# Later splits of the small products' operands and earlier w_out sums of odd pairs in a short-convolution block

## The chip, the cores and the metric

The kernel runs on one core of a Trainium2 chip. The metric is the device time of one execution in microseconds; runs are compared by their median. The profile comes from one execution that the hardware profiler recorded. TensorE (PE, and PEld for its weight loads) multiplies, VectorE (DVE) and ScalarE (ACT) work on SBUF and PSUM, GpSimd (POOL) works on SBUF alone, and SyncE (SP) issues nearly all DMAs. Each of them works through its own instructions in order.

## The reference

With DEPTH = 1 only the first layer, a gated short convolution between two norms, is computed, for 1024 positions of 1024 channels and an inner width of 2048, all in float32.

```python
def short_conv_mixer(u, w_in, conv_w, w_out):
    z, bg, cg, v = jnp.split(u @ w_in.astype(u.dtype), 4, axis=-1)
    y = bg * causal_dwconv(cg * v, conv_w) * jax.nn.silu(z)
    return y @ w_out.astype(u.dtype)
...
    u = rms_norm(h, pre_norm[i])
    m = short_conv_mixer(u, sc_w_in[j], sc_conv_w[j], sc_w_out[j])
    h = h + rms_norm(m, post_norm[i])
```

## The kernel before

Every float32 operand is split into a high and a low float32r part (`split`, L153: ScalarE copies the high part, VectorE subtracts to get the low part), and a product is three matmuls, low by high, high by low and high by high. The head normalises and transposes x into u. Then come the input projections, chunk by chunk. The 16 chunks of 128 inner channels give 32 **pairs** p: an even pair holds the columns of cg and v of chunk p // 2, an odd pair those of z and bg. One pair is a two by two block product, done with seven block products named a to g instead of eight. Each is 4 x 3 matmuls of 128x512 (L188 to L190). GpSimd makes the sums of weight blocks (`add_s`, L142 to L150), `split_w` splits them, and `after` combines the results: ScalarE copies a, c and e out of PSUM (`snap`, L196, tiles sna, snc, sne), and VectorE adds later products to them (L215 for d, L220 for f, L229 and L230 for g). Products a, g, c and d of one pair use one PSUM bank (px), so the next product on that bank waits until the snap of a has been read.

From chunk DEEP = 3 on (pair 6), the eighth product b is itself done with seven **small products** a' to g' (L684 to L686, 2 x 3 matmuls of 128x256) for the two pairs of a chunk together. Their u side is prepared once: `deep_parts` and `deep_subs` form sums on GpSimd, and `deep_split` splits them, c' with two copies and two subtractions of 128x256, and likewise e', d' and g'. This happens in the products of pairs 4 to 6, as the table `UNDER` (L755) says. Their weights come from `deep_sums` (GpSimd, L647 to L651) and `deep_prep` (tiles dw). `deep_after` (L695) adds a small product into sna; behind d' it calls `start_conv`, which multiplies into gpad (L236) and runs `conv`: one ScalarE copy (L578) and two VectorE sums of 128x1024 (L580).

The order of work is written out by hand in `slots` (L737). An even pair runs as c a' e b' d f c', then a of the next pair, e', g; an odd pair as c f' e d' d f g', then a of the next pair, g. Behind every product's matmuls the loop issues `prepare`, which splits the weights of the products that are due within LEAD = 7 us of a fixed table, then `after` or `deep_after`, then the DMAs and sums that belong to that product. An engine works in the order of this code, so a step's place in the loop is its place in its engine's queue.

Four sums of w_out (`add_t`, L278) are also made in this loop, for the output projection later. For each of eight row blocks, listed in `TODO` under the pairs 8, 10, 12, 13, 14, 15, 16 and 17, `fetch_t` (L272) loads four tiles t of 256 KB with four DMAs on SP. Four VectorE subtractions (L282, steps 0 to 3) follow, each with a store to DRAM (L283). In an even pair the loads stand behind c and all steps behind d. In an odd pair the loads stand behind c and the steps one by one behind d, f, the next a, and g:

```python
        if i in "dfag" and p % 2 != (i == "a") and p - (i == "a") in TODO:
            add_t(TODO[p - (i == "a")], ["dfag".index(i)])
```

Raw weights of pair p + 2 are fetched behind d (`fetch`, L130, four DMAs on SP). `y_done` (L243) stores a chunk of y behind g of an odd pair, on SP too. Pages of SBUF come from one pool of 36; a new tile takes a page that was freed earlier, and waits for it. The output projection, the second norm and the residual follow (L843 on).

Of the kernel before, what the change touches and what calls it, by code (L numbers as in the profile page):

```python
# [16 lines left out]
DEEP = 3  # L17
# [4 lines left out]
def kernel(  # L22
# [48 lines left out]
    def page(name, dtype=F32, shape=(HB,)):  # L71

        return pages.tile([P, *shape], dtype, tag="pg", name=name, bufs=PAGES)
# [79 lines left out]
    def split(src, hi, lo):  # L153
        nc.scalar.copy(hi, src)  # L154
        nc.vector.tensor_sub(lo, src, hi.bitcast(F32))  # L155
# [21 lines left out]
    def product(p, i, ks=None):  # L177

        w = wt[p, i]
        which = {"b": "y", "e": "v", "f": "v"}.get(i, "x")  # L180
        first = i in "abe"
        if first and (p, which) not in banks:
            banks[p, which] = bank(f"p{which}_{p}")
        ps = banks[p, which]
        for k in range(KH) if ks is None else ks:
            hi, lo = (h[:, k * P : (k + 1) * P] for h in w)
            last = k == KH - 1
            nc.tensor.matmul(ps, lo, UH[i][:, k], start=first and k == 0, stop=False, skip_group_check=True)  # L188
            nc.tensor.matmul(ps, hi, UL[i][:, k], start=False, stop=False, skip_group_check=True)  # L189
            nc.tensor.matmul(ps, hi, UH[i][:, k], start=False, stop=last, skip_group_check=True)  # L190
# [8 lines left out]
    def tap(c, j):  # L199
        i = j * NC + c  # L200
        return cw[:, i : i + 1]
# [30 lines left out]
            elif c < DEEP:  # L232
                start_conv(c)

    def start_conv(c):
        nc.vector.tensor_mul(gpad[:, TAPS - 1 : TAPS - 1 + HB], banks[2 * c, "x"], sn[2 * c, "a"])  # L236
        conv(c)


    done = {}  # L240
# [5 lines left out]
    def fetch_s(c):  # L246

        if c >= CH:
            ts = [page(f"s{e}_{c}") for e in (0, 1)]
            for e in (0, 1):  # L250
                nc.sync.dma_start(ts[e], y_d[:, c - CH, e * HB : (e + 1) * HB])
            done[c] = done[c], *ts
# [19 lines left out]
    def fetch_t(j):  # L272

        ts[j] = [page(f"t{n}_{j}") for n in range(4)]
        for n, t in enumerate(ts[j]):
            nc.sync.dma_start(t, wov[:, j + n // 2 * CH, n % 2 * HB : (n % 2 + 1) * HB])

    def add_t(j, steps=range(4)):  # L278

        t = ts[j]  # L280
        for n, a, b in [((1, 1, 0), (3, 3, 1), (0, 3, 0), (2, 2, 3))[n] for n in steps]:
            nc.vector.tensor_sub(t[n], t[a], t[b])  # L282
            nc.sync.dma_start(t_d[:, n, j], t[n])  # L283
# [289 lines left out]
    add_s(2, "ecdf")  # L573
    fetch(3)

    def conv(c):
        cv = tmp.tile([P, L], F32, tag="cv", name=f"cv_{c}")
        nc.scalar.activation(cv, gpad[:, :L], AF.Copy, scale=tap(c, 0))  # L578
        for j in range(1, TAPS):
            nc.vector.scalar_tensor_tensor(  # L580
                cv, gpad[:, j : j + L], tap(c, j), cv, op0=ALU.mult, op1=ALU.add
            )
        cvs[c] = cv
# [33 lines left out]
    def deep_subs(ks):  # L617

        for k in ks:
            (b11, b12), (b21, b22) = ((t[:, :HH], t[:, HH:]) for t in (deep[k], deep[k + KQ]))  # L620
            nc.gpsimd.tensor_sub(b12, b12, b11)
            nc.gpsimd.tensor_sub(b22, b22, b12)
            nc.gpsimd.tensor_sub(b11, b22, b11)
            nc.gpsimd.tensor_sub(b21, b21, b22)
# [3 lines left out]
    def deep_split(i):  # L628

        k0, l0 = DEEP_U[i]  # L630
        ls = slice(l0, l0 + HH)
        if i != "e'":
            deep[i] = [tmp.tile([P, KQ, HH], F32R, tag="ub", name=f"u{i[0]}{h}_deep", bufs=6) for h in "hl"]
        for k in range(KQ):
            if i == "e'":
                hi, lo = UH["b"][:, k, ls], UL["b"][:, k, ls]
            else:
                hi, lo = (t[:, k] for t in deep[i])
            split(deep[k0 + k][:, ls], hi, lo)

    def deep_sums(c, part):

        (a11, a12), (a21, a22) = ((t[:, :HH], t[:, HH:]) for t in (block(p, 0, 1) for p in (2 * c, 2 * c + 1)))
        t = page(f"ds{part}_{c}")
        deep[c, part] = t
        if part == 0:
            nc.gpsimd.tensor_add(t[:, :HH], a21, a22)  # L647
            nc.gpsimd.tensor_sub(t[:, HH:], t[:, :HH], a11)
        else:
            nc.gpsimd.tensor_sub(t[:, :HH], a11, a21)  # L650
            nc.gpsimd.tensor_sub(t[:, HH:], a12, deep[c, 0][:, HH:])  # L651
# [17 lines left out]
    def deep_product(c, i):  # L669

        n, off = DEEP_W[i]
        which = {"b'": "y'", "e'": "v'", "f'": "v'"}.get(i, "x'")
        first = i in ("a'", "b'", "e'")
        if first:
            banks[c, which] = bank(f"p{which[0]}2_{c}")
        ps = banks[c, which][:, :HH]
        for k in range(KQ):
            hi, lo = (h[:, off + k * P : off + (k + 1) * P] for h in deep_w[c, n])
            if i in deep:
                uh, ul = (t[:, k] for t in deep[i])  # L680
            else:
                kk, l0 = {"a'": (k, 0), "b'": (k + KQ, 0), "e'": (k, HH), "f'": (k + KQ, HH)}[i]
                uh, ul = (u["b"][:, kk, l0 : l0 + HH] for u in (UH, UL))
            nc.tensor.matmul(ps, lo, uh, start=first and k == 0, stop=False, skip_group_check=True)  # L684
            nc.tensor.matmul(ps, hi, ul, start=False, stop=False, skip_group_check=True)  # L685
            nc.tensor.matmul(ps, hi, uh, start=False, stop=k == KQ - 1, skip_group_check=True)  # L686
# [5 lines left out]
    def deep_after(c, i):  # L692
        which, row, half = DEEP_C[i]
        t = sn[2 * c + row, "a"][:, half * HH : (half + 1) * HH]
        nc.vector.tensor_add(t, banks[c, which][:, :HH], t)  # L695
        if i == "d'":
            start_conv(c)

# [33 lines left out]
    END = len(PAIRS) - 1  # L734
    TODO = {p: j for j, p in enumerate([8, 10, 12, 13, 14, 15, 16, 17])}

    slots = [("a", 2), ("b", 2)]  # L737
    for p in range(2, len(PAIRS)):
        q = p + 1
# [19 lines left out]
        ("f", 2 * DEEP - 2): lambda: deep_parts([3]),  # L759
        ("g", 2 * DEEP - 2): lambda: deep_subs([0]),  # L760
        ("c", 2 * DEEP - 1): lambda: deep_subs([1]),
        ("e", 2 * DEEP - 1): lambda: deep_split("c'"),
        ("d", 2 * DEEP - 1): lambda: deep_split("e'"),
        ("f", 2 * DEEP - 1): lambda: deep_split("d'"),
        ("a", 2 * DEEP): lambda: deep_split("g'"),
    }


# [7 lines left out]
    def prepare(n):  # L776
        while ready[0] < len(slots) and at[ready[0]] < at[n + 1] + LEAD:
            i, p = slots[ready[0]]
            if i[1:]:
                deep_prep(p, i)  # L780
            elif (p, i) not in wt:
                split_w(p, i)
            ready[0] += 1

    first_chunk("")
    for n, (i, p) in enumerate(slots):
        if i[1:]:
            deep_product(p, i)
            prepare(n)
            deep_after(p, i)  # L790
            if i == "g'":
                nc.scalar.activation(sn[2 * p + 1, "a"], sn[2 * p + 1, "a"], AF.Silu)
            continue
        product(p, i)
        prepare(n)
        after(p, i)
        q, prev = p + 1, p // 2 - 1
        if p == 2:
            first_chunk(i)
        if i == "c":  # L800
            if p % 2 and p // 2 < DEEP:
                nc.scalar.activation(sn[p, "a"], sn[p, "a"], AF.Silu)
            if p in TODO:
                fetch_t(TODO[p])
            if p % 2 == 0 and p > 2:
                fetch_s(prev)
            if p % 2 == 0 and p // 2 >= DEEP:
                deep_sums(p // 2, 1)
        elif i == "e":
            add_s(q, "ec")  # L810
        elif i == "d":
            if p + 2 <= END:
                fetch(p + 2)
            add_s(q, "d")
            if p in TODO and p % 2 == 0:
                add_t(TODO[p])
            if p % 2 == 0 and p > 2:
                add_y(prev)
        elif i == "f":
            add_s(q, "f")  # L820
            if p == 2:
                add_y(0)
        elif i == "g":
            if p % 2 and q <= END and q // 2 >= DEEP:
                deep_sums(q // 2, 0)
        if i in "dfag" and p % 2 != (i == "a") and p - (i == "a") in TODO:
            add_t(TODO[p - (i == "a")], ["dfag".index(i)])
        if DEEP < NC and (i, p) in UNDER:
            UNDER[i, p]()
        if p == END - 1 and i in "cd":  # L830
            fetch_unit()
        if p == END and i in "acdg":
            split_unit()
            fetch_unit()
# [153 lines left out]
```

## Time and profile before

| | before |
|---|---|
| median of 3 runs | 796.65 us (796.1 to 797.06) |
| profiled execution | 795.9 us, span 794.1 us |
| granted TensorE clock, mean | 0.997 |
| TensorE busy | 780.0 us (98%) |
| VectorE busy | 609.1 us (77%) |
| ScalarE busy | 334.6 us (42%) |
| GpSimd busy | 359.9 us (45%) |

A row of the timeline gives the start in us from the span's start, the time taken, the engine, the line, the operation, the tile written and those read, the shapes and the count; in brackets stands the engine's idle time before it and what ended that. Matmul rows overlap, since matmuls are pipelined and their ends are modelled. A row of the waits gives who waited for whom: us in total, times, the longest.

### The profile page before, as it was taken

To read this page: it belongs to the slowest core of one execution; us is meant where nothing else is said; L and a number is where in the kernel's file an instruction comes from. 1 tells how busy PE (TensorE), PEld (TensorE's weight loads), DVE (VectorE), ACT (ScalarE), POOL (GpSimd) and SP (SyncE) were. 2 spreads that over 40 slices of the span, in tenths; PEclk is the share of its full clock that TensorE was granted. 3 is DMA by queue.
4 is the path that set the end of the run, shared out by engine and by line. 5 is a ranking of instruction groups with operands and counts; after the bars stand their busy time and mean duration, and the time that the engine had idled before them with its cause. 6 is when DMAs were issued, how large, how long until landed. Compare 5 with 4: busy or idle time off the path is not lost.

```text
span 794.1 us, 10778 instructions
## 1 busy us (share of the span) xinstructions
PE 780.0 (98%) x3728; PEld 653.8 (82%) x3728; DVE 609.1 (77%) x832; ACT 334.6 (42%) x610; POOL 359.9 (45%) x257
## 2 busy tenths in 40 slices
PE   9999999999999999999999999999999999999996
PEld 7888888788888878787888888888888888888885
DVE  6899658968787879898976867787878867744766
ACT  8564433433434333334343434342434547554441
POOL 2616577747474654555555647373738100000020
PEclk9999999999999999999999999999999999999998
DMA  9110431316170818282615243332424559983037
GB/s 337 37 53 22 125 100 47 107 41 222 30 251 2 291 54 273 84 282 78 212 40 160 70 130 103 98 106 93 132 69 160 198 193 389 402 287 121 0 109 262
DMA packets 108325, 114.50 MB, mean 144 GB/s; under 512 B 6584, under 2 KB 72176, under 8 KB 108272
## 3 DMA queue, kind: packets, MB, share of 16 engines
q1 hardware_dynamic: 108256, 113.82, 43.2%
q8 instruction: 29, 0.48, 0.2%
q14 instruction: 24, 0.20, 0.1%
q10 hardware_dynamic: 16, 0.00, 0.0%
HBM read 84.44 MB, written 29.36 MB: 143 GB/s over the span
## 4 chain that ended last, share of the span: by engine, by line
PE 82%; DVE 8%; issue 3%; POOL 2%; DMA 2%; ACT 2%; DVEq 0%; SPq 0%; ACTq 0%; POOLq 0%
PE px L188 12%; PE px L189 12%; PE px L190 12%; PE pv L188 6%; PE pv L189 6%; PE pv L190 6%; PE po_x L865 3%; PE po_x L866 3%; PE po_x L864 3%; PE po_v L865 2%; PE po_v L866 2%; PE po_v L864 2%; PE px L686 1%; PE px L685 1%; PE px L684 1%
## 5 line engine op out<-in xcount | busy, mean ns | idle before, releaser
L217 POOL TENSOR_TENSOR sne<-sne,cv 128x512 f32<-128x512 f32 x15 | 24.8, 1653 | 156.6 <-DVE sne L215 140.9
L906 POOL TENSOR_TENSOR acc<-acc,xr 128x512 f32<-128x512 f32 x4 | 6.8, 1701 | 132.0 <-DVE acc L905 132.0
L580 DVE SCALAR_TENSOR_TENSOR cv<-gpad,cw,cv 128x1024 f32<-128x1024 f32 x32 | 41.9, 1308 | 19.0 <-ACT cv L578 18.5
L188 PE MATMUL px<-u_c,wcl 128*128 128x512 f32 x124 | 48.7, 393 | 4.5 <-ACT sna L196 4.5
L225 POOL TENSOR_TENSOR gpad<-snc,sne 128x512 f32<-128x512 f32 x15 | 20.1, 1338 | 71.6 <-DVE snc L220 71.6
L155 DVE TENSOR_TENSOR wel<-se,weh 128x512 fp32r<-128x512 f32 x31 | 49.9, 1611 | 3.2 <-ACT weh L154 3.2
L146 POOL TENSOR_TENSOR se<-raw,raw 128x512 f32<-128x512 f32 x31 | 50.6, 1631 | 2.8 <-DMA raw<-in_sc_w_in 2.4
L150 POOL TENSOR_TENSOR sf<-raw,sc 128x512 f32<-128x512 f32 x31 | 51.4, 1658 | 0.0
L148 POOL TENSOR_TENSOR sc<-se,raw 128x512 f32<-128x512 f32 x31 | 50.2, 1619 | 2.4
L196 ACT COPY sna<-px 128x512 f32<-128x512 f32 x30 | 17.5, 582 | 74.5 <-PE px L190 59.6
L188 PE MATMUL pv<-u_f,wfl 128*128 128x512 f32 x124 | 48.5, 391 | 0.3 <-DVE wfl L155 0.3
L188 PE MATMUL pv<-u_e,wel 128*128 128x512 f32 x124 | 48.6, 392 | 0.0
L189 PE MATMUL px<-u_d,wdh 128*128 128x512 f32 x124 | 48.6, 392 | 0.0
L188 PE MATMUL px<-u_a,wal 128*128 128x512 f32 x124 | 48.6, 392 | 0.0
L188 PE MATMUL px<-u_g,wgl 128*128 128x512 f32 x124 | 48.6, 392 | 0.0
L189 PE MATMUL pv<-u_e,weh 128*128 128x512 f32 x124 | 48.6, 392 | 0.0
L189 PE MATMUL px<-u_a,wah 128*128 128x512 f32 x124 | 48.6, 392 | 0.0
L188 PE MATMUL px<-u_d,wdl 128*128 128x512 f32 x124 | 48.6, 392 | 0.0
L189 PE MATMUL px<-u_g,wgh 128*128 128x512 f32 x124 | 48.5, 391 | 0.0
L189 PE MATMUL px<-u_c,wch 128*128 128x512 f32 x124 | 48.3, 390 | 0.0
L190 PE MATMUL pv<-u_f,wfh 128*128 128x512 f32 x124 | 48.3, 390 | 0.0
L190 PE MATMUL px<-u_c,wch 128*128 128x512 f32 x124 | 48.3, 390 | 0.0
(367 smaller groups left out, 2496.7 us busy)
## 6 DMA issues: line engine op xcount, KB each, us to landing
raw<-in_sc_w_in SPq DMA_DIRECT2D x128, 256.0 KB, 4.1
y_d<-cv SPq DMA_DIRECT2D x16, 512.0 KB, 3.0
s_d<-s SPq DMA_DIRECT2D x32, 256.0 KB, 2.4
t<-in_sc_w_out SPq DMA_DIRECT2D x32, 256.0 KB, 4.1
t_d<-t SPq DMA_DIRECT2D x32, 256.0 KB, 2.7
s<-y_d SPq DMA_DIRECT2D x16, 256.0 KB, 3.8
xr<-in_x SPq DMA_DIRECT2D x16, 256.0 KB, 4.7
xa<-in_x SPq DMA_DIRECT2D x4, 512.0 KB, 5.2
```

The costliest lines, as they stand in the source:

```text
L146: nc.gpsimd.tensor_add(t, block(p, 1, 0), block(p, 1, 1))
L148: nc.gpsimd.tensor_sub(t, sums[p, "e"], block(p, 0, 0))
L150: nc.gpsimd.tensor_sub(t, block(p, 0, 1), sums[p, "c"])
L155: nc.vector.tensor_sub(lo, src, hi.bitcast(F32))
L188: nc.tensor.matmul(ps, lo, UH[i][:, k], start=first and k == 0, stop=False, skip_group_check=True)
L189: nc.tensor.matmul(ps, hi, UL[i][:, k], start=False, stop=False, skip_group_check=True)
L190: nc.tensor.matmul(ps, hi, UH[i][:, k], start=False, stop=last, skip_group_check=True)
L217: nc.gpsimd.tensor_mul(t, t, cvs[c][:, HB:])
L580: nc.vector.scalar_tensor_tensor(cv, gpad[:, j : j + L], tap(c, j), cv, op0=ALU.mult, op1=ALU.add)
L864: nc.tensor.matmul(ps, lo, u[:, 0, k], start=first, stop=False, skip_group_check=True)
L865: nc.tensor.matmul(ps, hi, u[:, 1, k], start=False, stop=False, skip_group_check=True)
L866: nc.tensor.matmul(ps, hi, u[:, 0, k], start=False, stop=last, skip_group_check=True)
```

## The change

Two things move; nothing is added or removed, and the sums are the same.

The splits of the small products' operands: c' and e' move from behind e and d of pair 5 to behind a of pair 6, d' from behind f to behind g of pair 5, and g' from behind a to behind c of pair 6.

The w_out sums of odd pairs: the loads move from behind c of the pair to behind its a, which runs among the products of the pair before. Steps 0 and 1 move from behind d and f to behind f', step 2 from behind the next a into `conv`, between the ScalarE copy and the VectorE sums, and step 3 from behind g to behind g'. Even pairs keep their order.

```diff
@@ -232,9 +232,9 @@
-    def start_conv(c):
+    def start_conv(c, beside=lambda: None):
         nc.vector.tensor_mul(gpad[:, TAPS - 1 : TAPS - 1 + HB], banks[2 * c, "x"], sn[2 * c, "a"])
-        conv(c)
+        conv(c, beside)
@@ -573,9 +573,10 @@
-    def conv(c):
+    def conv(c, beside=lambda: None):
         cv = tmp.tile([P, L], F32, tag="cv", name=f"cv_{c}")
         nc.scalar.activation(cv, gpad[:, :L], AF.Copy, scale=tap(c, 0))
+        beside()
         for j in range(1, TAPS):
@@ -694,7 +695,7 @@
         if i == "d'":
-            start_conv(c)
+            start_conv(c, lambda: odd_t(2 * c + 1, [2]))
@@ -734,6 +735,10 @@
+    def odd_t(p, steps):
+        if p % 2 and p in TODO:
+            add_t(TODO[p], steps)
+
@@ -759,10 +764,9 @@
         ("c", 2 * DEEP - 1): lambda: deep_subs([1]),
-        ("e", 2 * DEEP - 1): lambda: deep_split("c'"),
-        ("d", 2 * DEEP - 1): lambda: deep_split("e'"),
-        ("f", 2 * DEEP - 1): lambda: deep_split("d'"),
-        ("a", 2 * DEEP): lambda: deep_split("g'"),
+        ("a", 2 * DEEP): lambda: (deep_split("c'"), deep_split("e'")),
+        ("g", 2 * DEEP - 1): lambda: deep_split("d'"),
+        ("c", 2 * DEEP): lambda: deep_split("g'"),
@@ -788,8 +792,11 @@
             deep_after(p, i)
-            if i == "g'":
+            if i == "f'":
+                odd_t(2 * p + 1, [0, 1])
+            elif i == "g'":
                 nc.scalar.activation(sn[2 * p + 1, "a"], sn[2 * p + 1, "a"], AF.Silu)
+                odd_t(2 * p + 1, [3])
             continue
@@ -800,7 +807,7 @@
-            if p in TODO:
+            if p % 2 == 0 and p in TODO:
                 fetch_t(TODO[p])
@@ -823,8 +830,9 @@
-        if i in "dfag" and p % 2 != (i == "a") and p - (i == "a") in TODO:
-            add_t(TODO[p - (i == "a")], ["dfag".index(i)])
+        elif i == "a":
+            if p % 2 and p in TODO:
+                fetch_t(TODO[p])
```

## The prediction

> **What bounds the kernel now.** I read the busy shares first, then TensorE's waits, then TensorE's own rows at those waits, and last VectorE's and ScalarE's order of work ahead of them.
>
> ```profile
> PE 780.0 (98%) x3728; PEld 653.8 (82%) x3728; DVE 609.1 (77%) x832; ACT 334.6 (42%) x610; POOL 359.9 (45%) x257
> PE px L188 <- ACT sna L196: 4.5, 4, 1.4
> PE pv L684 <- DVE sna L695: 0.6, 1, 0.6
> PE pv L188 <- DVE wfl L155: 0.3, 1, 0.3
> ```
>
> TensorE is busy 98% of the span, so an edit that touches no matmul can only win back TensorE's stops. The waits (total us, times, longest) list 4.5 + 0.6 + 0.3 = 5.4 us of them in the main loop. Here are the six places, and behind them two rows of a seam where nothing stopped:
>
> ```profile
> 140.33 0.50 PE L188 MATMUL px<-u_c,wcl 128*128 128x512 f32 x1 [1.40 <-ACT sna L196]
> 150.58 0.47 PE L188 MATMUL pv<-u_f,wfl 128*128 128x512 f32 x1 [0.31 <-DVE wfl L155]
> ...
> 293.43 0.50 PE L188 MATMUL px<-u_c,wcl 128*128 128x512 f32 x1 [1.08 <-ACT sna L196]
> 316.33 0.39 PE L684 MATMUL pv<-u_b,dw2l 128*128 128x256 f32 x1 [0.57 <-DVE sna L695]
> 333.42 0.50 PE L188 MATMUL px<-u_c,wcl 128*128 128x512 f32 x1 [1.03 <-ACT sna L196]
> 372.59 0.50 PE L188 MATMUL px<-u_c,wcl 128*128 128x512 f32 x1 [1.02 <-ACT sna L196]
> ...
> 410.36 0.39 PE L190 MATMUL px<-u_g,wgh 128*128 128x512 f32 x1
> 410.58 0.39 PE L188 MATMUL px<-u_c,wcl 128*128 128x512 f32 x1
> ```
>
> The unstopped seam shows matmuls of 0.39 us that start 0.22 apart. They overlap by 0.17, and a stop loses that overlap too; the first matmul after a stop is also about 0.1 longer (0.50 against 0.39). So each listed idle time is worth 0.17 + 0.11 = 0.28 more. The one at 140.33 cost 1.40 + 0.28 = 1.68; the three before products c of pairs 14, 16 and 18 cost 1.08 + 1.03 + 1.02 + 3 x 0.28 = 3.97; the one at 316.33 cost 0.57 + 0.28 = 0.85; the one at 150.58 cost 0.31 + 0.17 + 0.08 = 0.56. Together this is 7.06 us. That is all the change can win here: the remaining stops lie in the head and the tail, which it does not touch.
>
> **Part 1, the steps of w_out in odd pairs (13, 15, 17).** Pair 13 as it stands, VectorE first, then one row of GpSimd and two of ScalarE, and below the dots pair 19:
>
> ```profile
> 277.30 0.42 DVE L695 TENSOR_TENSOR sna<-pv,sna 128x256 f32<-128x256 f32 x1 [0.85 <-PE pv L686]
> 280.75 0.42 DVE L695 TENSOR_TENSOR sna<-px,sna 128x256 f32<-128x256 f32 x1 [2.02 <-PE px L686]
> 283.00 2.60 DVE L580 SCALAR_TENSOR_TENSOR cv<-gpad,cw,cv 128x1024 f32<-128x1024 f32 x2 [1.22 <-ACT cv L578]
> 286.72 0.68 DVE L282 TENSOR_TENSOR t<-t,t 128x512 f32<-128x512 f32 x1
> 289.63 1.18 DVE L282 TENSOR_TENSOR t<-t,t 128x512 f32<-128x512 f32 x1
> 290.73 0.41 DVE L695 TENSOR_TENSOR sna<-px,sna 128x256 f32<-128x256 f32 x1
> 286.89 1.67 POOL L217 TENSOR_TENSOR sne<-sne,cv 128x512 f32<-128x512 f32 x1 [10.99 <-DVE sne L215]
> 291.23 0.63 ACT L792 ACTIVATE sna<-sna 128x512 f32<-128x512 f32 x1 [0.86 <-DVE sna L695]
> 292.80 0.58 ACT L196 COPY sna<-px 128x512 f32<-128x512 f32 x1
> ...
> 406.32 0.41 DVE L695 TENSOR_TENSOR sna<-px,sna 128x256 f32<-128x256 f32 x1
> 408.13 0.69 DVE L155 TENSOR_TENSOR dw0l<-raw,dw0h 128x512 fp32r<-128x512 f32 x1 [1.40 <-ACT dw0h L154]
> 408.52 0.58 ACT L196 COPY sna<-px 128x512 f32<-128x512 f32 x1
> ```
>
> The first two t steps (286.72, 289.63) stand on VectorE between the convolution and the sum after g' (290.73). ScalarE's Silu (291.23) waits for that sum, the snap of a (292.80) stands behind the Silu, and product c at 293.43 waits for the snap, since both use one bank. The two steps hold the sum up by 0.6 and 1.1 us (to the starts of what follows them).
>
> The last three rows are the control, pair 19, which has no t step. Its g' sum is at 406.32 and its snap ends at 409.10, 1.48 us before its c starts at 410.58. VectorE's order after the change, from the d' sum to the g' sum, is that of pair 19 plus step 2. So I expect no stop at these three seams: gain 3.97. As a check, pair 13's snap ended at 293.38; without 1.7 us it ends at 291.7, and TensorE would reach c at 293.43 - 1.36 = 292.07, so 0.4 is left by the slower durations of pair 13.
>
> Where the steps go:
> - Steps 0 and 1, behind f' (after 277.30): VectorE has 2.02 idle before 280.75. At 0.6 each they take 1.2 of it: nothing on the path, and 0.8 is left. In pairs 15 and 17 that idle time is smaller now because VectorE runs late there; I take pair 13's, since what makes it late (next paragraph) goes too. Without the cover they would cost the excess over 2.02.
> - Step 2, between the convolution's copy and its sums: VectorE waits 1.22 for ScalarE there, the step takes 0.6: hidden, 0.5 left.
> - Step 3, behind g': VectorE then waits 1.40 for dw0h anyway (408.13). The step takes 0.68 to 1.18: hidden.
>
> The stop at 316.33 has another root. The even pair 14 waits for its own w_out rows:
>
> ```profile
> 299.65 0.32 SPq L243 DMA_DIRECT2D y_d<-cv  x1
> 301.74 1.81 SPq L276 DMA_DIRECT2D t<-in_sc_w_out  x4
> 307.00 0.69 DVE L282 TENSOR_TENSOR t<-t,t 128x512 f32<-128x512 f32 x1 [0.95 <-DMA t<-in_sc_w_out]
> 308.50 0.69 DVE L282 TENSOR_TENSOR t<-t,t 128x512 f32<-128x512 f32 x1 [0.81 <-DMA t<-in_sc_w_out]
> ```
>
> SP issues in order, and these loads stood behind the store of y, whose chunk VectorE finished late because steps 2 and 3 stood before it. Both steps are now earlier, so the store and the loads come several us sooner and the 0.95 + 0.81 of waiting goes. The stop was 0.57, less than this wait alone: gain 0.85.
>
> What moves on SP: an odd pair's t loads are issued at its product a instead of c, two products earlier. The price is that the four raw loads of pair 15 now stand behind the stores of steps 0, 1 and 2.
>
> ```profile
> 268.26 0.32 SPq L260 DMA_DIRECT2D s_d<-s  x1
> 269.95 1.76 SPq L276 DMA_DIRECT2D t<-in_sc_w_out  x4
> 271.80 5.05 SPq L130 DMA_DIRECT2D raw<-in_sc_w_in  x4
> 293.15 1.18 POOL L647 TENSOR_TENSOR ds<-raw 128x256 f32<-128x256 f32 x1
> DMA to landing us min/median/max: 2.8/3.9/5.3
> ```
>
> (The last row is for the t loads.) The t loads, now right behind the store at 268.26, or at worst at 269.95 as before, land between 272.5 and 277.0 (1.76 for the issues, up to 5.3 to land); step 0 wants them at 277.6. The raw loads slip from 271.80 to about 282.5, when step 2 is done, and land by some 290 with the same numbers. Their first reader is GpSimd at 293.15, perhaps 1.5 earlier after the change. Both hold, with 1 to 4 us in hand. Cost 0, bounded by 0 and the third rival below.
>
> **Part 2, the four splits.** The stretch around 140, VectorE and ScalarE:
>
> ```profile
> 130.38 1.84 DVE L155 TENSOR_TENSOR ucl_deep<-deep,uch_deep 128x256 fp32r<-128x256 f32 x2
> 133.35 1.84 DVE L155 TENSOR_TENSOR u_b<-deep,u_b 128x256 fp32r<-128x256 f32 x2
> 136.81 0.68 DVE L220 TENSOR_TENSOR snc<-pv,snc 128x512 f32<-128x512 f32 x1
> 137.53 0.63 ACT L222 ACTIVATE snc<-snc 128x512 f32<-128x512 f32 x1 [5.26 <-DVE snc L220]
> 138.49 2.78 DVE L155 TENSOR_TENSOR udl_deep<-deep,udh_deep 128x256 fp32r<-128x256 f32 x2 [0.99 <-ACT udh_deep L154]
> 139.71 0.57 ACT L196 COPY sna<-px 128x512 f32<-128x512 f32 x1
> 151.29 0.68 DVE L155 TENSOR_TENSOR wal<-raw,wah 128x512 fp32r<-128x512 f32 x1
> ```
>
> The splits c' and e' (1.84 each) stand before the sum of f (136.81); Silu, casts and the snap of a (139.71) follow it on ScalarE, and product c at 140.33 waits for the snap. Moved behind a, the 3.68 us are gone from in front. The sum can start when f's last matmul is done, near 133.5 to 134; the Silu and two casts end near 136, the snap near 136.8, against c's earliest start at 140.33 - 1.68 = 138.65. That leaves almost 2 us: the 1.68 comes back whole.
>
> But the splits do not vanish: c' and e' now stand behind a, d' behind g, g' behind c. VectorE works from 127 to past 155 with one idle time of 0.99 (at 138.49); the sum of its work up to the low part of the next a (wal, 151.29 to 151.97) is unchanged. New idle time, waiting for f's end and then for the casts, is at most some 2 us where 0.99 was, so wal ends between 151 and 153. TensorE wanted a at 154.0 (150.58, plus 12 matmuls of f and 6 half-sized ones of c' at 0.23 and 0.12); 2.24 earlier (1.68 + 0.56) is 151.8. So between 0 and 1.1 of the 2.24 is given back. I take 0.3, near the lower end, because GpSimd's work of this stretch moves forward as well, and VectorE's instructions are short (0.68) where GpSimd rests. Gain 1.9, bounds 1.1 and 2.24.
>
> On that length: the t step at 286.72 took 0.68 and began while GpSimd was still idle (its first instruction starts at 286.89); the one at 289.63 took 1.18, beside GpSimd's work. The Trainium skill (SBUF — State Buffer, Who interferes with whom) has a VectorE instruction with two SBUF inputs blocked, not slowed, while a GpSimd instruction reads SBUF. By that rule steps 0 and 1 would outgrow their cover wherever GpSimd works behind f'; rival 2 prices that from rows.
>
> **Sum.** 3.97 + 0.85 + 1.9 = 6.7 us. The list of TensorE's waits has no other entry behind 372.59, so nothing there waits for a fixed time and the gain reaches the end. The profiled execution took 795.9 (span 794.1 and 1.8 around it) and becomes 789.2; the median of the three runs, 796.65, lies 0.75 above it and becomes 796.65 - 6.7 = 789.95, say 790.0.
>
> **Rivals.**
> 1. The splits come back as late operands. wfl, the split of g' and wal stand in one queue, and a stop moves from c to the next f, c' or a. For it: VectorE was full here and already late once (150.58). Against: the idle time above. Gain 3.97 + 0.85 and little more, 4.8: 791.8. Chance 0.10.
> 2. Steps 0 and 1 are not covered. GpSimd is at work behind f' and each step is held for a whole instruction of it (1.67 at 286.89), so takes about 1.7: 3.4 instead of 1.2 against a cover of 2.02, so the d' sum, the convolution and the snap slip 1.4, about the 1.48 in hand in pair 19 and more than the 0.4 in hand in pair 13. About 1 us comes back at each seam: gain 6.7 - 3 = 3.7, time 793.0. Against: in pair 13 GpSimd rests for the 10.99 before 286.89, that is from 275.9 on. Chance 0.07.
> 3. Slower: the t loads are late at f'. VectorE runs in order, so waiting for them holds back the d' sum, the convolution and everything to the snap, three times. It decides when the last load lands more than 0.8 us after step 1's turn at 278.2. To eat 6.7 us and 1.6 more, each pair must lose 2.8, so landing at about 281.8, an issue near 276 instead of 270. That needs SP to be held for 6 us ahead of them, by a page not yet free or by the store of s. Then 798.3 or more. For it: SP was held by a late store at 299.65, and pair 14's loads took 5 us. Against: the loads move ahead, not back. Chance 0.06.
> 4. Nothing comes of it: another instruction ahead of the snaps takes the steps' place, within 1 us of 796.65. Against: pair 19. Chance 0.04.
>
> **How the numbers follow.** The forecast has 0.73; its own range goes from the full 7.06 to the low end of Part 2 (5.9), widened by the 0.55 between the median and the lowest run: 789.0 to 791.3. Rival 1 is next, with 0.5 of the same spread, then part of rival 2: the range is 789.0 to 792.6. A measurement of this kernel tells 0.2%, 1.6 us, from no change. Faster by more: the forecast and rivals 1 and 2, 0.90, less 0.02 for a mixture of them with 3, so 0.88. Within it: 0.05. Slower: 0.07.
>
> **What would show it.** Right: the waits no longer list c for the snap of a, nor f' for the sum; the seams before pairs 14, 16 and 18 run on at 0.22; no t step waits for a DMA; the t steps of odd pairs sit in the idle times before the d' sum, the convolution's sums and dw0l. Wrong: a t step with a DMA as releaser behind f', GpSimd waiting for raw, or a stop of TensorE at f, c' or a near 150.

## The result and the profile after

| | before | changed |
|---|---|---|
| median | 796.44 us (5 runs, 796.1 to 797.06) | 788.7 us (5 runs, 788.39 to 788.99) |
| profiled execution | 795.9 us, span 794.1 | 788.57 us, span 786.8 |

The ratio is 0.9901, with a 95% interval of 0.9887 to 0.9916. The change is 7.7 us faster, by that interval 6.7 to 9.0. The forecast was 790.0 in a range of 789.0 to 792.6: the direction held, and the gain came out larger than the range allowed.

The busy shares of the changed kernel's page, and all that its list of TensorE's waits has:

```profile
PE 778.4 (99%) x3728; PEld 654.3 (83%) x3728; DVE 601.8 (76%) x832; ACT 335.5 (43%) x610; POOL 362.6 (46%) x257
PE pw L321 <- DVE idle L287: 1.1, 1, 1.1
PE pk L345 <- DVE dg L420: 0.4, 1, 0.4
```

Both waits lie in the head. The waits for the snap of a (4.5 us before), for the sum that f' waits for and for f's weights have left the list. TensorE's own rows at the old stops, in the timeline of the changed kernel, with the low part of the next a's weights (wal) on VectorE between them:

```profile
138.40 0.39 PE L190 MATMUL px<-u_g,wgh 128*128 128x512 f32 x1
138.63 0.39 PE L188 MATMUL px<-u_c,wcl 128*128 128x512 f32 x1
...
148.04 0.39 PE L190 MATMUL px<-u_d,wdh 128*128 128x512 f32 x1
148.41 0.47 PE L188 MATMUL pv<-u_f,wfl 128*128 128x512 f32 x1
149.78 0.68 DVE L155 TENSOR_TENSOR wal<-raw,wah 128x512 fp32r<-128x512 f32 x1
151.91 0.39 PE L188 MATMUL px<-u_a,wal 128*128 128x512 f32 x1
...
289.74 0.39 PE L190 MATMUL px<-u_g,wgh 128*128 128x512 f32 x1
289.97 0.39 PE L188 MATMUL px<-u_c,wcl 128*128 128x512 f32 x1
```

At c of pair 6 (138.63) and c of pair 14 (289.97) the next matmul starts 0.23 after the last, as at a seam without a stop. At f of pair 6 (148.41) it starts 0.37 after and is 0.08 longer: of the 0.56 us there, 0.22 is left. Pair 13 on VectorE, then ScalarE, GpSimd and SP, and last pair 14's four sums on VectorE:

```profile
275.43 1.41 DVE L282 TENSOR_TENSOR t<-t,t 128x512 f32<-128x512 f32 x2
278.54 0.42 DVE L696 TENSOR_TENSOR sna<-px,sna 128x256 f32<-128x256 f32 x1 [0.76 <-PE px L687]
279.47 0.68 DVE L282 TENSOR_TENSOR t<-t,t 128x512 f32<-128x512 f32 x1
280.78 2.60 DVE L581 SCALAR_TENSOR_TENSOR cv<-gpad,cw,cv 128x1024 f32<-128x1024 f32 x2 [0.62 <-ACT cv L578]
285.70 0.42 DVE L696 TENSOR_TENSOR sna<-px,sna 128x256 f32<-128x256 f32 x1
286.03 0.86 DVE L282 TENSOR_TENSOR t<-t,t 128x512 f32<-128x512 f32 x1
287.52 1.08 DVE L155 TENSOR_TENSOR dw0l<-raw,dw0h 128x512 fp32r<-128x512 f32 x1 [0.63 <-ACT dw0h L154]
...
287.91 0.58 ACT L196 COPY sna<-px 128x512 f32<-128x512 f32 x1
...
291.41 1.18 POOL L648 TENSOR_TENSOR ds<-raw 128x256 f32<-128x256 f32 x1
...
266.46 1.85 SPq L276 DMA_DIRECT2D t<-in_sc_w_out  x4
280.60 2.11 SPq L130 DMA_DIRECT2D raw<-in_sc_w_in  x4
293.85 2.27 SPq L276 DMA_DIRECT2D t<-in_sc_w_out  x4
...
300.42 3.07 DVE L282 TENSOR_TENSOR t<-t,t 128x512 f32<-128x512 f32 x4
```

Every moved step sits in the idle time that was named for it. Steps 0 and 1 (275.43) leave 0.76 of the 2.02 before the d' sum, step 2 leaves 0.62 of the 1.22 at the convolution, and step 3 leaves 0.63 before dw0l. In pairs 15 and 17 the same idle times are left to 0.01 us. The snap ends at 288.49, 1.48 before c: pair 19's margin. The raw loads went out at 280.60 and GpSimd first reads them at 291.41. Pair 14's t loads go out 3.9 us after its c starts (293.85 against 289.97) instead of 8.3, and its sums (300.42) run without a wait.

### The profile page after: what moved, and what is told of

Its sections match the earlier page's. It is cut to its first block, busy times and chain, and to the rows that moved or that the text cites. A ratio compares the mean times of both kernels' runs of the same rounds, so it can differ in the third digit from the quotient of the medians.

```text
span 786.8 us, 10799 instructions
## 1 busy us (share of the span) xinstructions
PE 778.4 (99%) x3728; PEld 654.3 (83%) x3728; DVE 601.8 (76%) x832; ACT 335.5 (43%) x610; POOL 362.6 (46%) x257
## 4 chain that ended last, share of the span: by engine, by line
PE 98%; DVE 0%; DMA 0%; ACT 0%; issue 0%; DVEq 0%
PE px L188 14%; PE px L189 14%; PE px L190 14%; PE pv L188 7%; PE pv L189 7%; PE pv L190 7%; PE po_x L873 4%; PE po_x L872 4%; PE po_x L874 4%; PE po_v L873 2%; PE po_v L872 2%; PE po_v L874 2%; PE px L687 2%; PE px L685 2%; PE px L686 2%; PE pp L392 1%
## 5 line engine op out<-in xcount | busy, mean ns | idle before, releaser
L155 DVE TENSOR_TENSOR wel<-se,weh 128x512 fp32r<-128x512 f32 x31 | 52.2, 1683 | 3.2 <-ACT weh L154 3.2
L146 POOL TENSOR_TENSOR se<-raw,raw 128x512 f32<-128x512 f32 x31 | 52.2, 1684 | 3.6 <-DMA raw<-in_sc_w_in 3.1
L150 POOL TENSOR_TENSOR sf<-raw,sc 128x512 f32<-128x512 f32 x31 | 53.0, 1711 | 0.0
L196 ACT COPY snc<-px 128x512 f32<-128x512 f32 x31 | 18.2, 586 | 73.4 <-PE px L190 70.0
L188 PE MATMUL pv<-u_e,wel 128*128 128x512 f32 x124 | 48.6, 392 | 0.0
L188 PE MATMUL px<-u_g,wgl 128*128 128x512 f32 x124 | 48.5, 391 | 0.0
L188 PE MATMUL px<-u_a,wal 128*128 128x512 f32 x124 | 48.6, 392 | 0.0
L189 PE MATMUL px<-u_a,wah 128*128 128x512 f32 x124 | 48.6, 392 | 0.0
L188 PE MATMUL px<-u_d,wdl 128*128 128x512 f32 x124 | 48.5, 391 | 0.0
L189 PE MATMUL px<-u_g,wgh 128*128 128x512 f32 x124 | 48.4, 390 | 0.0
L188 PE MATMUL pv<-u_f,wfl 128*128 128x512 f32 x124 | 48.3, 390 | 0.0
L188 PE MATMUL px<-u_c,wcl 128*128 128x512 f32 x124 | 48.2, 389 | 0.0
L190 PE MATMUL px<-u_g,wgh 128*128 128x512 f32 x124 | 48.2, 389 | 0.0
L190 PE MATMUL px<-u_a,wah 128*128 128x512 f32 x124 | 48.2, 389 | 0.0
L190 PE MATMUL px<-u_c,wch 128*128 128x512 f32 x124 | 48.2, 389 | 0.0
```

The lines of the kernel that those rows point to most:

```text
L146: nc.gpsimd.tensor_add(t, block(p, 1, 0), block(p, 1, 1))
L150: nc.gpsimd.tensor_sub(t, block(p, 0, 1), sums[p, "c"])
L196: nc.scalar.copy(t, banks[p, "v" if i == "e" else "x"])
```

## The experiments

Each comes from the changed kernel unless it says otherwise. Its median is 788.7.

**Only the sums.** The splits stay where they were.

```diff
-        ("a", 2 * DEEP): lambda: (deep_split("c'"), deep_split("e'")),
-        ("g", 2 * DEEP - 1): lambda: deep_split("d'"),
-        ("c", 2 * DEEP): lambda: deep_split("g'"),
+        ("e", 2 * DEEP - 1): lambda: deep_split("c'"),
+        ("d", 2 * DEEP - 1): lambda: deep_split("e'"),
+        ("f", 2 * DEEP - 1): lambda: deep_split("d'"),
+        ("a", 2 * DEEP): lambda: deep_split("g'"),
```

> Only the w_out sums of odd pairs are moved; the four splits stay where they were. Theory (the gain is TensorE's stops, each worth its idle time plus 0.28 us, and the parts do not interact): the stops at 140.33 and 150.58 stay (1.68 and 0.56 us), the three before c of pairs 14, 16, 18 and the one at f' of pair 15 go, 4.8 us: about 4.8 to 5.2 us under the kernel before, 2.1 to 2.5 over the changed one. Rival (the surplus of the changed kernel over the sum of its stops comes from the sums, for instance from DMA or page waits that the list of waits does not show): 5.6 us or more under the kernel before.

790.74 us against 796.38 before (ratio 0.993, 0.9916 to 0.9943): 5.64 less. TensorE's waits in the loop:

```profile
PE px L188 <- ACT sna L196: 1.4, 1, 1.4
PE pv L188 <- DVE wfl L155: 0.3, 1, 0.3
```

The stops are exactly those foreseen. The gain by the medians is above the theory's 5.2 and at the rival's 5.6, but its interval, 4.5 to 6.7 us, holds both. The rows tell more. From the start of the first matmul of product c (L188) to that of the last, the loop takes 569.5 us here, and 574.5, 574.7 and 575.4 in three profiles of the kernel before (the second and third of these come below). That is 5.1 to 5.9 less: 4.2 for the three stops before c, and the rest are the stops at f', which differ from one execution to the next. So the surplus needs no wait that the list does not show.

**Only the splits.** The kernel before with the four splits moved.

```diff
-        ("e", 2 * DEEP - 1): lambda: deep_split("c'"),
-        ("d", 2 * DEEP - 1): lambda: deep_split("e'"),
-        ("f", 2 * DEEP - 1): lambda: deep_split("d'"),
-        ("a", 2 * DEEP): lambda: deep_split("g'"),
+        ("a", 2 * DEEP): lambda: (deep_split("c'"), deep_split("e'")),
+        ("g", 2 * DEEP - 1): lambda: deep_split("d'"),
+        ("c", 2 * DEEP): lambda: deep_split("g'"),
```

> Only the four splits are moved. Theory: the stop at c of pair 6 goes whole and the one at f shrinks to about 0.2: 2.0 to 2.2 us under the kernel before, and the stops of pairs 13 to 18 stay at their sizes. Rival (the surplus comes from the splits): 2.8 us or more under it.

794.08 us against 796.38 (0.9976, 0.9966 to 0.9986): 2.3 less, near the theory. The two parts add up, 5.64 + 2.3 = 7.94 against 7.74. But its profiled execution took 795.04, near the upper end of 793.48 to 795.52, and its waits show part of the reason:

```profile
PE px L188 <- ACT sna L196: 3.1, 3, 1.1
PE pv L684 <- DVE sna L695: 1.2, 2, 0.8
```

At f' there are now two stops, 1.2 us, where the first profile of the kernel before had one of 0.6. Nothing in this edit touches them. Whether they differ from one execution to the next is tested on the kernel before, below.

**Steps 0 and 1 back.** They stand behind d and f again, steps 2 and 3 behind g'.

```diff
-            start_conv(c, lambda: odd_t(2 * c + 1, [2]))
+            start_conv(c)
-            if i == "f'":
-                odd_t(2 * p + 1, [0, 1])
-            elif i == "g'":
+            if i == "g'":
-                odd_t(2 * p + 1, [3])
+                odd_t(2 * p + 1, [2, 3])
+        if i in "df":
+            odd_t(p, ["df".index(i)])
```

> The changed kernel with steps 0 and 1 of odd pairs behind d and f again, steps 2 and 3 together behind g'. Theory (steps 0 and 1 between the convolution and the sum of g' hold up the snap of a): the stops before c of pairs 14, 16, 18 come back with 1.2 to 1.4 us each, 3.6 to 4.2 together: about 792.5. Rival (step 2 beside the convolution and the general lateness of VectorE made those stops): they stay away or come back with under 0.5 each, under 790.2.

792.89 us, 4.2 over the changed kernel. The first row is its waits, the second its timeline at c of pair 14, the third and fourth pair 14's t loads and sums:

```profile
PE px L188 <- ACT sna L196: 3.1, 3, 1.0
291.46 0.50 PE L188 MATMUL px<-u_c,wcl 128*128 128x512 f32 x1 [1.02 <-ACT sna L196]
298.61 2.20 SPq L276 DMA_DIRECT2D t<-in_sc_w_out  x4
304.98 2.02 DVE L282 TENSOR_TENSOR t<-t,t 128x512 f32<-128x512 f32 x3 [0.72 <-DMA t<-in_sc_w_out]
```

The three stops are back, at 1.02 + 0.28 as in the kernel before. Steps 0 and 1 in front of the sum of g' are their cause. The stop at f' stayed away.

**Steps 2 and 3 back.** Step 2 is behind the next a, step 3 behind g.

```diff
-            start_conv(c, lambda: odd_t(2 * c + 1, [2]))
+            start_conv(c)
-                odd_t(2 * p + 1, [3])
+        if i == "a":
+            odd_t(p - 1, [2])
+        elif i == "g":
+            odd_t(p, [3])
```

> The changed kernel with step 2 behind the next a and step 3 behind g again; steps 0 and 1 stay behind f'. As the prediction put it (steps 2 and 3 before the store of y make pair 14's loads late, and that makes the stop of 0.85 us at f' of pair 15): the wait of pair 14's sums for their loads comes back, with it a stop of up to 0.85 us, about 789.5. Rival (that stop came from the stops before it, which let VectorE's backlog pile up; without them pair 14 has room for late loads): no stop, within 0.2 us of the changed kernel.

788.42 us (788.24 to 788.79): the rival. No TensorE wait in the loop, no t step that waits for a DMA. Pair 14's loads and sums:

```profile
294.41 0.34 SPq L243 DMA_DIRECT2D y_d<-cv  x1
295.93 1.87 SPq L276 DMA_DIRECT2D t<-in_sc_w_out  x4
302.04 2.73 DVE L282 TENSOR_TENSOR t<-t,t 128x512 f32<-128x512 f32 x4
```

The four sums run through without a wait. So moving steps 2 and 3 bought nothing that steps 0 and 1 had not. The loads go out 6.2 us after c of pair 14 (which starts at 289.70), where the kernel before has 8.3. With steps 0 and 1 back, as above, they went out 7.15 us after it, and the wait of 0.72 made no stop. Only with both halves in their old places was the wait long enough for a stop.

**The loads behind c again.**

```diff
-            if p % 2 == 0 and p in TODO:
+            if p in TODO:
                 fetch_t(TODO[p])
-        elif i == "a":
-            if p % 2 and p in TODO:
-                fetch_t(TODO[p])
```

> The changed kernel, but an odd pair's t loads are issued behind c again, two products later. Theory (between a and c SP has nothing else to issue, so only the pages that the loads take change; loads issued some 2 us later still land near the moment step 0 wants them): no stop of TensorE, within 0.3 us of the changed kernel, with waits of the t steps for their DMA of at most 0.5 us in pairs 15 and 17. Rival (the slower case of the prediction: VectorE stands before late loads behind f' and holds back the convolution): waits of 2 us or more behind f', stops before c again, 1 to 4 us slower than the changed kernel.

788.64 us, the changed kernel's time, without a wait for t. Pair 13's loads went out here:

```profile
267.50 1.76 SPq L276 DMA_DIRECT2D t<-in_sc_w_out  x4
```

That is 1 us later than in the changed kernel, and they were in time. Moving the loads gained nothing and cost nothing.

**The cover behind f'.** Two, then five more subtractions behind steps 0 and 1, in pairs 13, 15 and 17; their result is not used.

```diff
                 odd_t(2 * p + 1, [0, 1])
+                if 2 * p + 1 in TODO:
+                    more = page(f"more_{p}")
+                    for _ in range(2):
+                        nc.vector.tensor_sub(more, ts[TODO[2 * p + 1]][3], ts[TODO[2 * p + 1]][1])
```

> The changed kernel with two extra subtractions of the same shape behind steps 0 and 1 in pairs 13, 15 and 17 (their result is not used). Theory (0.76 us of idle time are left before the d' sum and 1.48 between the snap's end and c): two cost 1.2 to 1.4 us, the d' sum slips by about 0.6, c does not wait: within 0.3 us of the changed kernel. Rival (anything more behind f' goes straight to TensorE): 1.8 us slower or more.

> The same with five extra subtractions. Theory: 3.1 to 3.4 us, less 0.76 of idle time and 1.48 in hand leaves 0.9 to 1.2 per seam, plus 0.28 for each stop: 3.5 to 4.4 us slower than the changed kernel, with three stops before c for the snap of a. Rival (the cover is larger than these rows say): under 1 us slower.

With two: 788.91 us, as the theory said, and no stop. With five: 793.71, 5.0 over, where 3.5 to 4.4 was expected. The waits with five:

```profile
PE px L188 <- ACT sna L196: 2.6, 3, 0.9
PE px L188 <- DVE sne L215: 0.7, 2, 0.4
```

The stops before c are there (2.6 and three times 0.28, 3.4 in all). The expectation missed a second stop: g also waits, for VectorE to have read d out of the bank (sne). By its matmuls' starts that costs 0.3, 0.6 and 0.6 in the three pairs. The cover is as the rows say; the seam has two deadlines behind it, not one.

**Only c' and e' moved.**

```diff
-        ("a", 2 * DEEP): lambda: (deep_split("c'"), deep_split("e'")),
-        ("g", 2 * DEEP - 1): lambda: deep_split("d'"),
-        ("c", 2 * DEEP): lambda: deep_split("g'"),
+        ("a", 2 * DEEP): lambda: (deep_split("c'"), deep_split("e'"), deep_split("g'")),
+        ("f", 2 * DEEP - 1): lambda: deep_split("d'"),
```

> The changed kernel with c' and e' of the splits behind a of pair 6, but d' behind f of pair 5 and g' behind a of pair 6 as before. Theory (the sum of f goes ahead, so c of pair 6 no longer waits; but the splits of d' and g', up to 2.9 and 1.8 us, again stand before the low part of f's weights, while TensorE comes to f 1.7 us sooner): no stop at c, a stop of 1.5 to 2 us at f of pair 6, so nearly all of the 2.1 us of the splits' gain is lost: 1.2 to 1.8 us slower than the changed kernel. Rival (moving c' and e' out of the way of the sum is all that counts): within 0.4 us of the changed kernel.

792.43 us, 3.7 over the changed kernel. The stop at c is gone and another has come, as the theory said, but one product earlier and larger, and it costs more than its length. VectorE's two rows ahead of the stop, the stop and what follows it, then three stretches around it (length; busy times of PE, PEld, DVE, ACT and POOL; granted clock; DMA share and GB/s):

```profile
144.14 2.92 DVE L155 TENSOR_TENSOR ugl_deep<-deep,ugh_deep 128x256 fp32r<-128x256 f32 x2
146.98 0.68 DVE L155 TENSOR_TENSOR wdl<-raw,wdh 128x512 fp32r<-128x512 f32 x1
...
147.81 0.47 PE L188 MATMUL px<-u_d,wdl 128*128 128x512 f32 x1 [2.17 <-DVE wdl L155]
...
149.02 0.63 PE L189 MATMUL px<-u_d,wdh 128*128 128x512 f32 x1
149.45 0.63 PE L190 MATMUL px<-u_d,wdh 128*128 128x512 f32 x1
...
145.12:148.53 3.41, 1.24 (x8) 0.99 (x7) 3.38 (x5) 1.99 (x4) 1.65 (x2) 1.00 0.00 0
148.53:151.94 3.41, 3.41 (x9) 2.67 (x9) 3.41 (x7) 0.62 (x1) 0.00 (x0) 0.50 0.59 179
151.94:155.35 3.41, 3.41 (x18) 2.85 (x17) 2.22 (x5) 0.00 (x0) 0.00 (x0) 1.00 1.09 328
```

The stop is for d's weights (wdl), behind the split of g' (ugl_deep, 2.92 us). It is worth 2.17 + 0.25, and then the matmuls start 0.43 apart instead of 0.23 for 3.4 us, at a granted clock of 0.50: eight of them, 1.6 us more.

**The kernel before, profiled twice more.**

> The kernel before, unchanged, for a second profile. What is looked for: why its median lies 0.5 us above its profiled execution and its executions spread over 1.9 us, where those of the changed kernel spread over 0.6. Theory (the stops at f' of pairs 15 and 17 hang on when pair 14's and 16's t loads land, and that differs from one execution to the next): the four stops before c and the one at f of pair 6 repeat within 0.1 us, and the stops at f' differ from those of the first profile (0.85 and 0), by 0.3 us or more in one of them. Rival (the difference is the granted clock or the head): all six stops repeat within 0.1 us.

> The same once more: the stops before c repeat, those at f' may not; the time follows the sum of the f' stops.

796.18 and 796.59 us. The waits of the first of these profiles, then its t sums in pairs 14 and 16:

```profile
PE px L188 <- ACT sna L196: 4.5, 4, 1.4
PE pv L684 <- DVE sna L695: 0.4, 1, 0.4
306.77 0.69 DVE L282 TENSOR_TENSOR t<-t,t 128x512 f32<-128x512 f32 x1 [0.57 <-DMA t<-in_sc_w_out]
308.15 2.02 DVE L282 TENSOR_TENSOR t<-t,t 128x512 f32<-128x512 f32 x3 [0.69 <-DMA t<-in_sc_w_out]
347.97 2.02 DVE L282 TENSOR_TENSOR t<-t,t 128x512 f32<-128x512 f32 x3 [1.43 <-DMA t<-in_sc_w_out]
```

And of the second:

```profile
PE px L188 <- ACT sna L196: 4.5, 4, 1.4
PE pv L684 <- DVE sna L695: 1.1, 2, 0.8
306.66 0.69 DVE L282 TENSOR_TENSOR t<-t,t 128x512 f32<-128x512 f32 x1 [0.68 <-DMA t<-in_sc_w_out]
308.12 2.02 DVE L282 TENSOR_TENSOR t<-t,t 128x512 f32<-128x512 f32 x3 [0.77 <-DMA t<-in_sc_w_out]
348.41 2.02 DVE L282 TENSOR_TENSOR t<-t,t 128x512 f32<-128x512 f32 x3 [2.09 <-DMA t<-in_sc_w_out]
```

The four waits for the snap repeat to 0.1 us; the waits for the t loads do not, and the stops at f' follow them. By the starts of the matmuls, and with the longer first matmul, these stops cost 0.85 us in the first profile (pair 15 alone), 0.36 + 0.64 in the second and 0.56 + 1.09 in the third. Each is what the sums of the pair before waited for their loads, less 0.8 to 1.0 us: in pair 14 they waited 1.76, 1.26 and 1.45 us, in pair 16 0.58 (no stop), 1.43 and 2.09.

The loop follows these stops: 574.5, 574.7 and 575.4 us from the first matmul of c to its last, and 573.7 in each without them. The whole times, 795.9, 796.18 and 796.59, follow less closely, because the head differs too: over all fourteen profiles of this document the first product c starts between 45.8 and 46.7 us. In these three, 173.3 us follow the start of the last one.

**The even pairs' loads earlier.** The kernel before, with one edit.

```diff
-            if p in TODO:
+            if p % 2 and p in TODO:
                 fetch_t(TODO[p])
+        elif i == "a":
+            if p % 2 == 0 and p in TODO:
+                fetch_t(TODO[p])
```

> The kernel before with one edit: the t loads of even pairs are issued at product a of the pair instead of c, so ahead of the odd pair's last steps and of the store of y on SP. Steps and splits stay where they were. Theory (late loads of the even pairs make the stops at f', and these vary): the stops at f' of pairs 15 and 17 go, those before c stay; 0.8 to 1.4 us under the kernel before, with a spread of at most 0.9 us. Rival (the f' stop comes from VectorE's backlog after the stop before c): the stop stays, within 0.3 us of the kernel before.

795.27 us against 796.57 (0.9985, 0.9976 to 0.9994): 1.3 less. In its profile no t step waits and the stops at f' are gone:

```profile
PE px L188 <- ACT sna L196: 4.6, 4, 1.4
PE pv L188 <- DVE wfl L155: 0.3, 1, 0.3
```

So these stops cost 1.3 us by the medians (0.5 to 1.9 by the interval), not the 0.85 of one profile. The loop confirms it: 573.7 us, what the kernel before takes without its stops at f'. The spread shrank from 2.1 us to 1.17, where 0.9 at most was expected. The start of the first product c, which no edit here touches, differs by as much as 0.9 between profiles, and can make most of what is left.

**d' and g' later still**, behind c and e of pair 6.

```diff
-        ("g", 2 * DEEP - 1): lambda: deep_split("d'"),
-        ("c", 2 * DEEP): lambda: deep_split("g'"),
+        ("c", 2 * DEEP): lambda: deep_split("d'"),
+        ("e", 2 * DEEP): lambda: deep_split("g'"),
```

> The changed kernel with two splits still later: d' behind c of pair 6 and g' behind e of pair 6. Theory (the last stop in the loop, 0.22 us at f of pair 6, is the low part of f's weights behind the split of d'): that stop goes and none comes in its place, 0.2 us under the changed kernel by the profile, not told apart by the times. Rival (the splits now make the weights of c' or of the next a late): a new stop of 0.3 us or more at c' or a of pair 7.

789.04 us (788.81 to 789.34), not told apart from the changed kernel. In its timeline the last stop in the loop is gone (f starts 0.23 after d's last matmul), and none came in its place:

```profile
148.66 0.39 PE L190 MATMUL px<-u_d,wdh 128*128 128x512 f32 x1
148.89 0.39 PE L188 MATMUL pv<-u_f,wfl 128*128 128x512 f32 x1
```

No version was found that beats the changed kernel beyond the spread of its runs.

## Why the prediction was right and where it was wrong

**The stops before c, right, a little low.** 3.97 was forecast. Steps 0 and 1 alone bring them back (4.2 us by the times), and pair 19 was the right control: after the change pair 13 has its margin of 1.48, not the 0.4 of the prediction's check. By the starts of the same matmuls in the first profile of the kernel before and in that of the changed kernel, the changed kernel's lead grows by 1.43, 1.39 and 1.40 us across the three stops, 4.2 in all. So a stop costs 0.35 to 0.38 us more than its listed idle time (0.31 with steps 0 and 1 back), not 0.28: the matmuls behind it start some 0.01 us further apart for a while. Why they do is open.

**The splits, right, a little low, and partly by luck.** 1.9 was forecast, with 0.3 given back out of a possible 1.1. By the same starts their move gave 2.1, and by the times of that part alone 2.3. The prediction looked for the loss at the next a, with wal ending between 151 and 153. There nothing was lost: wal ends at 150.46, and a starts at 151.91. What was given back is the 0.22 at f, whose stop the prediction had counted as won back whole. That 0.3 and 0.22 lie close is luck. That the work returns as late operands is real, as the run with only c' and e' moved shows: d' and g' had to go as well.

**The wait of pair 14, wrong in size and in part in cause.** This is the step of the sum that failed. The prediction took the 0.85 of the one profiled execution. The stop is not a constant: it depends on when four DMAs land, in two pairs, and pair 16's wait, which the profile listed at 0.58 with no stop behind it, makes one in other executions. The three profiles have 0.85, 1.00 and 1.65, and removing it was worth 1.3 by the medians. That late loads make it held, as the run with the even pairs' loads earlier shows. The cause of their lateness was named as steps 2 and 3 before the store of y; they are one of two conditions, and putting them back changes nothing.

**The ceiling of the sum, wrong.** "All the change can win here", 7.06, was the total of one execution that was faster than each of the five runs in the table (795.9 against 796.1 to 797.06; later runs of that kernel lie between 795.23 and 797.33). The range's low end then allowed for the runs' spread, but not for stops that are longer in most runs, nor for a price per stop that was too low. With 2.1 for the splits, 4.2 before c and 0.85 to 1.65 at f' the sum is 7.1 to 8.0, and that is what the loop lost: 574.5, 574.7 or 575.4 less 567.4. The measured 7.7 lies within. The differences that remain are smaller than what the head alone varies by.

**The places of the steps and the costs put at nothing, right.** The later raw loads cost nothing. The earlier t loads are not needed. The slower rival did not come. Nor did rival 2: GpSimd rested behind f' (10.99 us, up to 284.67 in pair 13), and steps 0 and 1 took 1.41 together in all three pairs. What they would have cost behind f' with GpSimd at work is not shown, since no run here has it so.

## What to carry to other kernels

A sum of stops from one profile holds for the stops that engines make for each other, since these repeat to 0.1 us; a stop behind a DMA wait is a draw, so take two or three profiles, or the spread of the times, before its size goes into a sum or sets a ceiling. The time of a stretch from one product's start to another's leaves out what differs in the head, and told here what the medians could not. A like stage without the step (pair 19) is the best measure of what moving the step out will give. When work is put off, follow the next deadlines of the same queue: it came back at the next weights, at a bank that had yet to be read, and nowhere only where idle time was found for all of it.

## What the runs showed of the hardware

In the run with only c' and e' moved, a stop of TensorE of 2.17 us was followed by a granted clock of 0.50 for 3.41 us (148.53 to 151.94). The drop set in 0.7 us after work had resumed. The 1.40 us before c in the kernel before had no such effect: its granted clock is 1.00 over 135 to 151, and the matmuls behind the stop start 0.23 to 0.24 apart.

In each of the fourteen traces the changes of the granted clock lie whole multiples of 3.413 us apart (42, 1 and 186 of them in the run with the drop). On this grid the stop of 2.17 (145.64 to 147.81) lies wholly in the window 145.12 to 148.53, at whose end the clock dropped and in which TensorE was busy for 1.24 of 3.41 us. The window of the kernel before that holds its 1.40, 137.69 to 141.10, has 2.02 us busy, and no drop followed. That the share of such a window decides is an inference from these two.

The drop also seems to differ between executions: four of the five runs with that stop have a mean clock of 0.995 or 0.996 and take 792.3 to 793.1 us; the fifth has 0.998 and takes 790.9, as it would without the drop, but it has no profile. The Trainium skill (TensorE: Matmul & The Clock Gate, Part 1: The HAM clock gate) puts the slow state behind at least one idle window of about 3.4 us, free-running. The length of the drop and the spacing of the changes agree; the window ahead of this drop was idle for 2.17 us of its 3.41 only.

An f32 subtraction of 128x512 took 0.68 alone and 0.86 behind g', beside GpSimd. In the kernel before, beside GpSimd, it took 1.18 at 289.63 and 1.78 at 339.54.
